# Recurrence of a hybrid decoder layer: loads two chunks ahead, outputs made in loaded tiles, one operand layout for both heads

## The chip, the cores and the metric

The kernel runs on one core of a Trainium2 chip. The metric is the device time of one execution in microseconds (us), the smaller the better. The engines are named as in the profile: PE multiplies matrices, DVE and ACT work on vectors, POOL and SP here mostly issue DMAs. Each engine runs its own list of instructions in order, and semaphores make it wait for the others.

## The reference

One layer of a decoder: token mixing by two branches (RWKV-7 and S5), gated and merged, then an MLP. Sequence 1024, model width 1024, float32. The change is in the RWKV-7 branch, with 8 heads of 64 channels:

```python
def step(S, inp):
    r_t, w_t, k_t, v_t, a_t, b_t = inp
    sa = jnp.einsum('bhij,bhj->bhi', S, a_t)
    S = (S * w_t[:, :, None, :] + sa[..., None] * b_t[:, :, None, :]
         + v_t[..., None] * k_t[:, :, None, :])
    return S, jnp.einsum('bhij,bhj->bhi', S, r_t)
...
y = ((y - mean) * lax.rsqrt(var + LNX_EPS)).reshape(bsz, L, RWKV_WIDTH) * lnx_w + lnx_b
bonus = jnp.sum(rh * kh * r_k, axis=-1, keepdims=True) * vh
y = (y + bonus.reshape(bsz, L, RWKV_WIDTH)) * g
```

## The kernel before

**Chunks.** The recurrence is computed in chunks i = 0 to 3. A chunk is half of the sequence (th = i // 2) for four heads (g = i % 2, as two pairs u = 0, 1), cut into 8 blocks of 64 steps. A chunk goes through these stages, which the text calls by name and number, as in level(1):

- rwkv_front: for each pair u SP and POOL load k, the decay, the rate and r (L693), ACT and DVE form the operands ar, bk and the decay products (L697 to L732), PE forms the block products (L743), DVE masks them into the tile gr (L745), and POOL stores parts of gr to DRAM (md, L751).
- rwkv_inv: POOL loads md as the tile mt (L795), DVE inverts the 32x32 triangles in 31 steps of two instructions (L802 writes tm, L804 the tile x), and POOL stores x (xd, L807) and loads it into gr (L814).
- rwkv_nat: PE transposes bk and v for the chain (L774 to L784).
- rwkv_level: the two 32x32 triangles of a block become one of 64x64. DVE transposes out of gr into a tile xz (L826), PE multiplies (L829, L831), ACT copies back (L830 into xz, L832 into gr).
- rwkv_chain: eight steps one after the other, L859 to L902, each a round of small matmuls with DVE and ACT between them.
- rwkv_out: normalisation (L933 to L943), PE transposes back, factors are loaded (L926), ACT scales (L951), DVE adds and multiplies (L954).

**Fill.** PE does not wait for this: between the pieces it gets matmuls of 128x512 of the projections (L176, L177, L178, three passes for one product, called fill below). In order these are tiles of the gates, then the merge of the first half of the sequence, which needs the outputs of chunks 0 and 1, the output projection, and the gated unit of the S5 branch. Each weight is cast on ACT (L159) and DVE (L160).

**Order.** `drive` (L200 on) runs generators, the lanes, and hands out fill when none is due: chain_lane (L1981) with nat, level, chain and out, prep_lane (L1959) for u = 0 and 1 with front and inv, and glu_lane. Each yields a cost and a due time or a condition, from the table of T constants at L2020. PE keeps the order in which this program writes its instructions. The other engines' lists are ordered by the priorities of the lanes and when operands are planned to be ready. A front of chunk i is started when rwkv_nat(i-1) has been issued.

**Tiles.** Pool "ld" has NLD = 10 places, shared by loaded tiles, the factors, the outputs and xz. The tile x of the inversion has one place, so a second x waits until the first has been stored and read.

```python
x = self.tg("x", 1, (128, 2, 8, 32), pool=self.rka)
...
xz = self.tg("ld", NLD).rearrange("p (u c t) -> p u c t", u=2, t=32)
...
yield 0, lambda: self.nat >= i - 1
```

Of the kernel before, what the change touches and what calls it, by code (L numbers as in the profile page):

```python
# [42 lines left out]
_o = 0  # L43
for _n, _c in (("ident", 128), ("gmask", 192), ("ones_bd", 128), ("nrow", 128),
               ("xinit", 256), ("smask", 512)):
    CST[_n] = (_o, _c)
    _o += _c
# [3 lines left out]
def _constants():  # L51
    c = np.zeros((128, NCST), np.float32)

    def put(name, a):
        o, n = CST[name]
        c[:, o:o + n] = a
    p = np.arange(128)
    put("ident", np.eye(128))
    s, t = (p % 64)[:, None], (p % 64)[None, :]
    g = np.where(p[None, :] < 64, s < t, s <= t)  # L60
    put("gmask", np.concatenate([g, g[:, 0:64]], axis=1))
    put("ones_bd", (p[:, None] // 64) == (p[None, :] // 64))
    put("nrow", np.broadcast_to(p[None, :], (128, 128)))
    x = np.zeros((128, 8, 32))
    for lane in range(128):
        for i in range(8):
            x[lane, i, 4 * i + lane // 32] = 1
    put("xinit", x.reshape(128, 256))
    put("smask", np.broadcast_to((np.arange(512) % 64 != 0)[None, :], (128, 512)))
    return c  # L70


class Kern:
# [591 lines left out]
    def rwkv_tiles(self, d, g, th):  # L665
        d.update(g=g, th=th)
        pool = self.rk if g else self.rka
        d["ar"] = self.tg("ar", 1, (128, 2, 8, 128), pool=pool)
        d["bk"] = self.tg("bk", 1, (128, 2, 8, 128), pool=self.rka)
        d["gr"] = self.tg("gr", 1, (128, 2, 8, 2, 128), pool=pool)  # L670
# [5 lines left out]
    def rwkv_front(self, d, u):  # L676

# [3 lines left out]
        p = 2 * d["g"] + u  # L681
        ar, bk = d["ar"][:, u], d["bk"][:, u]
        ar0, ar1, bk0, bk1 = [[x[HS[h], :, HS[h ^ j]] for h in range(2)] for x in (ar, bk) for j in range(2)]

        gf = d["gr"][:, u].rearrange("p c h t -> p (c h t)")
# [12 lines left out]
        if d["g"] == d["th"] == 0:  # L698
            self.tc.add_manual_dep(self.squared.ins, self.last_wh.ins.name, ORDER)
        yield 0, T_LD  # L700
        st = self.rp((128, 4, 2))
        for tb in range(4):
# [12 lines left out]
        G.tensor_copy(d["pt"][:, :, u], pe[:, :, 64])  # L715
        tk = self.tg("ld", NLD)
        A.activation(tk, ta, AF.Identity, bias=self.ka_1[:, p:p + 1], scale=self.ka_h[:, p:p + 1])
        V.tensor_tensor(tk, tk, k, ALU.mult)
        for h, sl in enumerate(HS):
            V.tensor_tensor(ar1[h], c64(r)[sl], pe[sl, :, 1:65], ALU.mult)  # L720
            V.tensor_tensor(bk1[h], c64(tk)[sl], c64(tz)[sl], ALU.mult)
        yield 0.9, T_KN, 1.5
        kb = self.rp()
# [11 lines left out]

        gm = [self.cst("gmask")[:, x].unsqueeze(1).to_broadcast([128, 4, 128]) for x in (slice(0, 128), slice(64, 192))]
        for q in range(2):
# [6 lines left out]
            for h in range(2):  # L744
                V.tensor_tensor(d["gr"][:, u, 4 * q:4 * q + 4, h], ps[h], gm[h], ALU.mult)  # L745
            yield 1.8, T_GR
        for blk in range(2):
            md = d["md"][u, blk].rearrange("(c h) q t -> h q c t", h=2)
            for h in range(2):
                sl = slice(64 * h + 32 * blk, 64 * h + 32 * blk + 32)  # L750
                nc.gpsimd.dma_start(md[h], d["gr"][sl, u, :, h, sl])  # L751

        V.scalar_tensor_tensor(r, r, self.vec("r_k", p), tk, ALU.mult, ALU.mult)
        pb = self.rp()
# [34 lines left out]
    def rwkv_inv(self, d):  # L789
# [19 lines left out]
        for u in range(2):  # L809
            for blk in range(2):  # L810
                xd = xds[16 * blk:16 * blk + 16, u].rearrange("(c h) s r t -> h (s r) c t", h=2)
                for h in range(2):
                    sl = slice(64 * h + 32 * blk, 64 * h + 32 * blk + 32)
                    nc.gpsimd.dma_start(d["gr"][sl, u, :, h, sl], xd[h])  # L814

    def rwkv_level(self, d):
# [5 lines left out]
        p0, p1 = [p0[:, u] for u in range(2)], [self.chb().rearrange("p (c t) -> p c t", t=32) for u in range(2)]  # L822
        xz = self.tg("ld", NLD).rearrange("p (u c t) -> p u c t", u=2, t=32)
        top, bot = [[slice(64 * h + o, 64 * h + o + 32) for h in range(2)] for o in (0, 32)]
        for h, sl in enumerate(top):
            self.levelled = V.transpose(xz[sl].rearrange("p u c t -> p (u c) t"), gr[sl, :, :, h, sl].rearrange("p u c t -> p (u c) t"))  # L826
        yield 0, T_LT
        kw = dict(stop=True, skip_group_check=True)
        steps = ((lambda u, c, h: mm(p1[u][bot[h], c], gr[top[h], u, c, h, bot[h]], xz[top[h], u, c], start=c == 0, **kw),  # L829
                  lambda u, h: A.copy(xz[bot[h], u], p1[u][bot[h], 0:8])),  # L830
                 (lambda u, c, h: mm(p0[u][top[h], c], xz[bot[h], u, c], gr[bot[h], u, c, h, bot[h]], start=c == 0, **kw),  # L831
                  lambda u, h: A.copy(gr[top[h], u, :, h, bot[h]], p0[u][top[h], 0:8])))  # L832
        for step, evict in steps:
# [10 lines left out]
    def rwkv_chain(self, d):  # L844
# [5 lines left out]
        kw = dict(stop=True, skip_group_check=True)  # L850
        uh = [(u, h, HS[h], HS[1 - h]) for u in range(2) for h in range(2)]

        def banks():
# [3 lines left out]
        def values(pg, c, u):  # L857
            for _, h, sl, ot in uh[0:2]:
                mm(pg[sl, u], gr[ot, u, c, h, sl], UV[ot, (c + h) % 8, h, u], start=u == 0, **kw)  # L859

# [9 lines left out]
        for c in range(8):  # L870
# [4 lines left out]
            for u in range(2):  # L875
                for _, h, sl, ot in uh[0:2]:
                    mm(pa[sl, u], ar[sl, u, c, sl], S[sl, u], start=u == 0, **kw)
                if c < 7:
# [8 lines left out]
            for u, h, sl, ot in uh:  # L887
                mm(pu[sl, u], gr[sl, u, c, h, sl], p1[sl, u], start=u == 0, **kw)
            for u, h, sl, ot in uh:
                mm(py[ot, u], ar[sl, u, c, ot], S[sl, u], start=c == 7 and u == 0, **kw)  # L890
            V.tensor_copy(UV[0:64, c, 0], pu[0:64])
            A.copy(UV[64:128, (c + 1) % 8, 1], pu[64:128])
            yield 0.45, T_CH
            for u, h, sl, ot in uh:
                mm(py[ot, u], gr[:, u, c, h, ot], UV[:, (c + h) % 8, h, u], start=False, **kw)
            o = 64 * (c % 2)
# [17 lines left out]
    def rwkv_out(self, d):  # L914
# [4 lines left out]
        final = th == 1 and d["g"] == 1  # L919
        ts = []  # L920

        def factors(u):
            r = []
            for src in (d["bv"][u], self.TG[2 * d["g"] + u][:, o]):
                t = self.tg("ld", NLD)
                (G if final else nc.sync).dma_start(t, src)  # L926
# [978 lines left out]
    def front_half(self):  # L1905
# [26 lines left out]
        with tc.tile_pool(reuse_waits="tile", name="rk", bufs=1) as self.rk, tc.tile_pool(reuse_waits="tile", name="evb", bufs=NEV) as self.evp, \  # L1932
# [5 lines left out]
            self.leveling, self.masked = False, 0.0  # L1938
            self.fronts = 0
            mg, self.mx0 = [], []  # L1940
# [18 lines left out]
    def prep_lane(self, u):  # L1959
        for i, d in enumerate(self.ds):  # L1960
            yield 0, lambda: self.nat >= i - 1
            if not d:
                self.rwkv_tiles(d, i % 2, i // 2)
            yield from self.rwkv_front(d, u)
            self.fronts += 1
# [15 lines left out]
    def chain_lane(self, mg):  # L1981
# [4 lines left out]
        for i, d in enumerate(self.ds):  # L1986
# [41 lines left out]
NLD = 10  # L2028
# [82 lines left out]
```

## Time and profile before

| | |
|---|---|
| median of 3 runs | 1575.64 us (1575.17 to 1583.24) |
| profiled execution | 1575.62 us, span of the core 1573.8 us |
| busy DVE, ACT, POOL | 1163.3 us (74%), 731.2 us (46%), 181.1 us (12%) |
| granted PE clock, mean | 0.965 of full speed |
| DMA | 224.46 MB, 143 GB/s on the mean |

A profile row reads: engine, line, what is written <- what is read, count, and then busy time. Times in windows and rows are from the start of the span. `[3.59 <-ACT hh L241]` behind a row means that the engine was idle 3.59 us before it, and that ACT's line 241 ended that wait. PE is busy for most of the span, and the recurrence takes the stretch from about 260 to 800 us.

### The profile page before, as it was taken

How to read it: one execution, taken by the hardware profiler on the slowest of the kernel's cores; microseconds unless marked ns; L12 is line 12 of the kernel's file. 1: busy time of each engine (PE TensorE's matmuls, PEld its weight loads, DVE VectorE, ACT ScalarE, POOL GpSimd, SP SyncE). 2: the span in 40 equal slices, each digit the busy share in tenths (PEclk: the TensorE clock that was granted, in tenths of full speed). 3: DMA queues.
4: the chain of work that ended last, by engine and by line, in shares of the span. 5: the costliest groups of instructions: out<-in, count | busy, mean ns of one | idle time of the engine just before them, and what ended most of it. 6: DMA issues, size and time to landing. Idle time of an engine off the chain costs nothing.

```text
span 1573.8 us, 23463 instructions
## 1 busy us (share of the span) xinstructions
PE 1485.4 (94%) x8608; PEld 1196.8 (76%) x8608; DVE 1163.3 (74%) x2130; ACT 731.2 (46%) x1206; POOL 181.1 (12%) x340
## 2 busy tenths in 40 slices
PE   6997999999998989799799999999999999999995
PEld 5786888878676767567578788888888888788774
DVE  7878874747365568786467869788888887698677
ACT  5454543332344365357534546455555555444350
POOL 0022110132221121303100011000000000000000
PEclk9998999999998998899779999999999999999997
DMA  6454344443333174435425666333333336943722
GB/s 198 122 148 131 101 138 131 149 131 115 103 96 137 62 238 143 140 81 169 134 69 193 208 235 200 107 120 103 118 108 114 121 112 203 333 162 129 235 65 107
DMA packets 121123, 224.46 MB, mean 143 GB/s; under 512 B 30976, under 2 KB 37120, under 8 KB 121008
## 3 DMA queue, kind: packets, MB, share of 16 engines
q1 hardware_dynamic: 90144, 154.02, 31.1%
q0 software_dynamic: 21024, 64.71, 12.3%
q10 hardware_dynamic: 9840, 4.24, 1.0%
q8 instruction: 67, 1.10, 0.3%
q14 instruction: 48, 0.39, 0.1%
HBM read 163.41 MB, written 57.41 MB: 140 GB/s over the span
## 4 chain that ended last, share of the span: by engine, by line
PE 71%; DVE 11%; DMA 9%; issue 5%; ACT 3%; SPq 1%; POOL 0%; DVEq 0%; ACTq 0%; POOLq 0%
PE gm L176 10%; PE gm L177 9%; PE gm L178 9%; PE rp L1541 5%; PE rp L1543 5%; PE rp L1542 5%; DMA st<-in_w_down_dram 3%; PE mm L1541 2%; PE mm L1543 2%; PE mm L1542 2%; PE d L1719 1%; PE d L1720 1%; PE d L1718 1%; DVE wl L242 1%; DVE wl L160 1%
## 5 line engine op out<-in xcount | busy, mean ns | idle before, releaser
L176 PE MATMUL gm<-hh,wh 128*128 128x512 f32 x688 | 290.3, 422 | 9.5 <-ACT hh L241 7.1
L177 PE MATMUL gm<-hl,wh 128*128 128x512 f32 x688 | 274.2, 399 | 1.4 <-DVE hl L242 1.2
L178 PE MATMUL gm<-hh,wl 128*128 128x512 f32 x688 | 272.8, 396 | 0.0
L159 ACT CAST wh<-wf 128x512 fp32r<-128x512 f32 x178 | 109.7, 620 | 189.6 <-PE gm L177 111.1
L160 DVE TENSOR_TENSOR wl<-wf,wh 128x512 fp32r<-128x512 f32 x178 | 122.7, 692 | 73.8 <-ACT wh L159 72.8
L176 PEld LDWEIGHTS gm<-hh,wh 128*128 128x128 f32 x688 | 131.7, 191 | 43.3 <-ACT hh L241 9.3
L178 PEld LDWEIGHTS gm<-hh,wl 128*128 128x128 f32 x688 | 131.9, 192 | 28.7
L177 PEld LDWEIGHTS gm<-hl,wh 128*128 128x128 f32 x688 | 132.1, 192 | 27.8 <-DVE hl L242 5.2
L1719 PE MATMUL d<-xl,wh 128*128 128x512 f32 x308 | 120.4, 391 | 5.3 <-DVE xl L242 5.3
L1718 PE MATMUL d<-xh,wh 128*128 128x512 f32 x308 | 120.1, 390 | 0.0
L1720 PE MATMUL d<-xh,wl 128*128 128x512 f32 x308 | 119.9, 389 | 0.0
L1541 PE MATMUL rp<-t,h 128*128 128x512 f32 x252 | 98.3, 390 | 1.6 <-ACT p L1555 1.6
L1542 PE MATMUL rp<-t,h 128*128 128x512 f32 x252 | 98.1, 389 | 0.0
L1543 PE MATMUL rp<-t,l 128*128 128x512 f32 x252 | 98.0, 389 | 0.0
L1719 PEld LDWEIGHTS d<-xl,wh 128*128 128x128 f32 x308 | 57.8, 188 | 19.3 <-DVE xl L242 7.4
L242 DVE TENSOR_TENSOR l<-r,h 128x1024 fp32r<-128x1024 f32 (+1 forms) x40 | 38.9, 972 | 40.0 <-ACT h L241 40.0
L241 ACT CAST h<-r 128x1024 fp32r<-128x1024 f32 (+1 forms) x40 | 34.0, 849 | 72.3 <-PE rp L1542 67.2
L1720 PEld LDWEIGHTS d<-xh,wl 128*128 128x128 f32 x308 | 57.8, 188 | 11.9
L1718 PEld LDWEIGHTS d<-xh,wh 128*128 128x128 f32 x308 | 57.8, 188 | 11.9
L1562 DVE SCALAR_TENSOR_TENSOR y<-zv,vecs,y 128x1023 f32<-128x1023 f32 (+1 forms) x42 | 53.8, 1281 | 10.2 <-ACT y L1560 10.2
L1541 PEld LDWEIGHTS rp<-t,h 128*128 128x128 f32 x252 | 47.3, 188 | 12.2 <-ACT p L1555 2.4
L1543 PEld LDWEIGHTS rp<-t,l 128*128 128x128 f32 x252 | 47.3, 188 | 9.9
(457 smaller groups left out, 3370.3 us busy)
## 6 DMA issues: line engine op xcount, KB each, us to landing
r<-in_w_up_dram SPq DMA_DIRECT2D x42, 512.0 KB, 3.7
wf<-in_w_in_dram SPq DMA_DIRECT2D x72, 256.0 KB, 3.0
st<-in_w_down_dram SPq DMA_DIRECT2D x55, 256.0 KB, 4.7
st<-ACT SPq DMA_DIRECT2D x44, 256.0 KB, 4.4
ACT<-y POOLq DMA_DIRECT2D x21, 512.0 KB, 2.9
GT<-ev POOLq DMA_DIRECT2D x32, 256.0 KB, 3.4
wf<-in_w_br_dram SPq DMA_DIRECT2D x32, 256.0 KB, 3.5
wf<-in_w_out_dram SPq DMA_DIRECT2D x32, 256.0 KB, 2.9
```

Of the source, the lines that this page charges most:

```text
L159: self.last_wh = nc.scalar.copy(h[:, :n], f[:, :n])
L160: nc.vector.tensor_tensor(l[:, :n], f[:, :n], h[:, :n].bitcast(F32), ALU.subtract)
L176: mm(ps, a, xh[k], start=a0, stop=False)
L177: mm(ps, a, xl[k], start=False, stop=False)
L178: mm(ps, b, xh[k], start=False, stop=z0)
L242: self.split_ops = a, (eng or self.nc.vector).tensor_tensor(lo, x, hi.bitcast(F32), ALU.subtract)
L1541: mm(ps, wh[:, c], xh, start=first and k == 0, stop=False, skip_group_check=True)
L1542: mm(ps, wh[:, c], xl, start=False, stop=False, skip_group_check=True)
L1543: mm(ps, wl[:, c], xh, start=False, stop=k == 3, skip_group_check=True)
L1718: mm(ps, wh[:, c], xh[:, x], start=start, stop=False, skip_group_check=True)
L1719: mm(ps, wh[:, c], xl[:, x], start=False, stop=False, skip_group_check=True)
L1720: mm(ps, wl[:, c], xh[:, x], start=False, stop=stop, skip_group_check=True)
```

## The change

1. **Loads.** A front's loads and its first squares are issued when chain(i-2) has been issued (new counter `chains`), and not when nat(i-1) has. The rest of the front still waits for nat(i-1), and for the outputs of chunk i-2, whose loaded factors now lie in the tile ar. For chunks 0 and 1 the new load condition holds from the start.
2. **Operands.** ar and gr have the same column order for both heads, so that the products at L720 and L729 take one instruction for 128 partitions in place of two for 64. The mask is one of 128 columns. The product r*r_k*tk stands earlier, and tk lies in a part of gr in place of a tile of "ld".
3. **Outputs.** Factors are loaded into the dead ar (or "ld") before the transposes, and two DVE instructions read the transposed PSUM tile, add and multiply in place. The scaling on ACT (L951) is gone.
4. **Level.** xz takes the tile x of the inversion (one place) in chunks 0 to 2.
5. **Due times.** T_KN 17 to 12, T_BK 13 to 10, T_INV 62 to 58.

```diff
     def rwkv_tiles(self, d, g, th):
...
+    def rwkv_operands(self, d):
+        d["ar"] = self.tg("ar", 1, (128, 2, 8, 128), pool=self.rk if d["g"] else self.rka)
+        d["bk"] = self.tg("bk", 1, (128, 2, 8, 128), pool=self.rka)
...
         yield 0, T_LD
+        yield 0, lambda: self.nat >= i - 1 and self.outs >= i - 1
+        if "ar" not in d:
+            self.rwkv_operands(d)
...
-        tk = self.tg("ld", NLD)
+        tk = yb
...
+        V.tensor_tensor(ar1, c64(r), pe[:, :, 1:65], ALU.mult)
         for h, sl in enumerate(HS):
-            V.tensor_tensor(ar1[h], c64(r)[sl], pe[sl, :, 1:65], ALU.mult)
             V.tensor_tensor(bk1[h], c64(tk)[sl], c64(tz)[sl], ALU.mult)
+        V.scalar_tensor_tensor(r, r, self.vec("r_k", p), tk, ALU.mult, ALU.mult)
...
-        for h, sl in enumerate(HS):
-            V.scalar_tensor_tensor(ar0[h], c64(kk)[sl], -1.0, pe[sl, :, 0:64], ALU.mult, ALU.mult)
+        V.scalar_tensor_tensor(ar0, c64(kk), -1.0, pe[:, :, 0:64], ALU.mult, ALU.mult)
...
-        V.scalar_tensor_tensor(r, r, self.vec("r_k", p), tk, ALU.mult, ALU.mult)
...
-        xz = self.tg("ld", NLD).rearrange("p (u c t) -> p u c t", u=2, t=32)
+        xz = (self.tg("ld", NLD) if d["g"] and d["th"] else self.tg("x", 1, pool=self.rka)).rearrange("p (u c t) -> p u c t", u=2, t=32)
...
-                t = self.tg("ld", NLD)
+                t = self.tg("ld", NLD) if final or d["g"] > j else free[:, (2 if u == 0 else 0) + j]
...
-            sq = self.tg("ld", NLD, (128, 8, 64))
+            sq = free[:, j].rearrange("p (a i) -> p a i", i=64)
...
+        if not final:
+            ts = [factors(u) for u in range(2)]
         yield 0, T_LF if final else T_LN
...
-            y1 = self.tg("ld", NLD)
-            A.activation(y1, ps.rearrange("p c t -> p (c t)"), AF.Identity, bias=self.vec("lnx_b", p),
-                         scale=self.vec("lnx_w", p))
-            for t, op in zip(ts[u] if final else factors(u), (ALU.add, ALU.mult)):
-                V.tensor_tensor(y1, y1, t, op)
+            y1, tg = ts[u]
+            V.scalar_tensor_tensor(y1, ps.rearrange("p c t -> p (c t)"), self.vec("lnx_w", p), y1, ALU.mult, ALU.add)
+            V.scalar_tensor_tensor(y1, y1, self.vec("lnx_b", p), tg, ALU.add, ALU.mult)
...
     def prep_lane(self, u):
         for i, d in enumerate(self.ds):
-            yield 0, lambda: self.nat >= i - 1
+            yield 0, lambda: self.chains >= i - 1
...
             yield from self.rwkv_chain(d)
+            self.chains = i + 1
...
-T_KN, T_BK, T_GR, T_INV, T_LV, T_CH, T_LN, T_LF = 17.0, 13.0, 2.5, 62.0, 1.0, 0.8, 16.0, 14.5
+T_KN, T_BK, T_GR, T_INV, T_LV, T_CH, T_LN, T_LF = 12.0, 10.0, 2.5, 58.0, 1.0, 0.8, 16.0, 14.5
```

The first place where the order moves is DVE's list around level(0). Before, the inversion of chunk 0 ends with the last write of x_3158, and the two transposes of level(0) (L826, into the tile ld_3781) follow inside the operands of front(1):

```order
596 L802 TENSOR_TENSOR tm_3254<-x_3158,mt_3157 128x16
...
598 L804 TENSOR_TENSOR x_3158<-x_3158,tm_3254 128x16
...
608 L160 TENSOR_TENSOR wl_3797<-wf_3798,wh_3796 128x512
609 L826 STREAM_TRANSPOSE ld_3781<-gr_2606 32x512
610 L732 SCALAR_TENSOR_TENSOR bk_3355<-gr_3356,ld_3371 64x8x64
611 L826 STREAM_TRANSPOSE ld_3781<-gr_2606 32x512
612 L732 SCALAR_TENSOR_TENSOR bk_3355<-gr_3356,ld_3371 64x8x64
```

After the change, DVE's list at the same stage (the transposes of level are L830 now; x_3109 and x_3695 are the inversions of chunks 0 and 1, tm and mt their operands, x_3828 and x_4637 the tiles xz of levels 0 and 1; L885 is the first step of chain(0)):

```order
609 L807 TENSOR_TENSOR x_3109<-x_3109,tm_3205 128x16
...
614 L749 TENSOR_TENSOR gr_3024<-rp_3638,csts 128x4x128
...
619 L805 TENSOR_TENSOR tm_3701<-x_3695,mt_3694 128x62
...
680 L807 TENSOR_TENSOR x_3695<-x_3695,tm_3791 128x16
681 L830 STREAM_TRANSPOSE x_3828<-gr_2604 32x512 x2
...
683 L830 STREAM_TRANSPOSE x_4637<-gr_3024 32x512 x2
684 L713 SCALAR_TENSOR_TENSOR ld_4534<-csts,ld_4534 128x512
...
686 L885 TENSOR_TENSOR p_797_3980<-p_797_3980,chk_3982 128x128
```

The whole of front(1) and of the inversion of chunk 1 now stands ahead of level(0)'s transposes, where before they stood behind them, and the transposes of level(1) and a scan of chunk 2 (L713) stand ahead of chain(0).

The second place is PE's list in the fourth and fifth step of the last chain, chain(3). Before, the steps (chk, chb and p are a step's products, S the state, UV the values) follow each other with nothing between:

```order
2760 L888 MATMUL chb_7927<-p_1509_7899,gr_5878 64x64 x4
2761 L890 MATMUL chk_7926<-S_2601,ar_5876 64x64 x4
2762 L895 MATMUL chk_7926<-UV_7355,gr_5878 64x64 x4
2763 L900 MATMUL chb_7927<-UV_7355,bkn_7354 64x64 x4
2764 L877 MATMUL chk_7964<-S_2601,ar_5876 64x64 x2
2765 L859 MATMUL chk_7964<-UV_7355,gr_5878 64x64 x2
...
2768 L888 MATMUL chb_7965<-p_1513_7937,gr_5878 64x64 x4
```

After the change, in the same chain (L882, L864, L893, L895, L900 and L905 are its products now; gm_7746 and gm_7803 are fill):

```order
2669 L882 MATMUL chk_7768<-S_2601,ar_5729 64x64 x2
2670 L864 MATMUL chk_7768<-UV_6999,gr_5588 64x64 x2
...
2673 L176 MATMUL gm_7746<-e_7152,wh_7737 128x512
2674 L177 MATMUL gm_7746<-e_7153,wh_7737 128x512
2675 L178 MATMUL gm_7746<-e_7152,wl_7738 128x512
...
2679 L893 MATMUL chb_7769<-p_1430_7705,gr_5588 64x64 x4
2680 L895 MATMUL chk_7768<-S_2601,ar_5729 64x64 x4
...
2687 L900 MATMUL chk_7768<-UV_6999,gr_5588 64x64 x4
```

Fill now stands between all products of that chain. From the first product of chain(3) to its end there are 210 fill matmuls in place of 96; counted from the start of the recurrence's fill, nat(0) stands at fill 957 in place of 993, level(0) at 1164 in place of 1233, chain(0) at 1200 in place of 1269 and chain(3) at 1965 in place of 2151, of 2892 in all.

More of the change, by code (lines that the diff above doesn't have):

```diff
@@ L43 @@
 _o = 0
-for _n, _c in (("ident", 128), ("gmask", 192), ("ones_bd", 128), ("nrow", 128),
+for _n, _c in (("ident", 128), ("gmask", 128), ("ones_bd", 128), ("nrow", 128),
                ("xinit", 256), ("smask", 512)):
@@ L60, in _constants @@
     g = np.where(p[None, :] < 64, s < t, s <= t)
-    put("gmask", np.concatenate([g, g[:, 0:64]], axis=1))
+    put("gmask", g)
     put("ones_bd", (p[:, None] // 64) == (p[None, :] // 64))
@@ L666, in rwkv_tiles @@
         d.update(g=g, th=th)
[L667 to L670, printed above, removed]
+        d["gr"] = self.tg("gr", 1, (128, 2, 8, 2, 128), pool=self.rk if g else self.rka)
         d["v"] = {}
@@ L681, in rwkv_front @@
         p = 2 * d["g"] + u
-        ar, bk = d["ar"][:, u], d["bk"][:, u]
-        ar0, ar1, bk0, bk1 = [[x[HS[h], :, HS[h ^ j]] for h in range(2)] for x in (ar, bk) for j in range(2)]
         gf = d["gr"][:, u].rearrange("p c h t -> p (c h t)")
@@ L700, in rwkv_front @@
         yield 0, T_LD
+        yield 0, lambda: self.nat >= i - 1 and self.outs >= i - 1
+        if "ar" not in d:
+            self.rwkv_operands(d)
+        ar, bk = d["ar"][:, u], d["bk"][:, u]
+        ar0, ar1 = ar[:, :, 0:64], ar[:, :, 64:128]
+        bk0, bk1 = [[bk[HS[h], :, HS[h ^ j]] for h in range(2)] for j in range(2)]
         st = self.rp((128, 4, 2))
@@ L734, in rwkv_front @@
         yield 0.5, T_BK
-        gm = [self.cst("gmask")[:, x].unsqueeze(1).to_broadcast([128, 4, 128]) for x in (slice(0, 128), slice(64, 192))]
+        gm = self.cst("gmask").unsqueeze(1).to_broadcast([128, 4, 128])
         for q in range(2):
@@ L744, in rwkv_front @@
             for h in range(2):
-                V.tensor_tensor(d["gr"][:, u, 4 * q:4 * q + 4, h], ps[h], gm[h], ALU.mult)
+                V.tensor_tensor(d["gr"][:, u, 4 * q:4 * q + 4, h], ps[h], gm, ALU.mult)
             yield 1.8, T_GR
@@ L822, in rwkv_level @@
         p0, p1 = [p0[:, u] for u in range(2)], [self.chb().rearrange("p (c t) -> p c t", t=32) for u in range(2)]
-        xz = self.tg("ld", NLD).rearrange("p (u c t) -> p u c t", u=2, t=32)
+        xz = (self.tg("ld", NLD) if d["g"] and d["th"] else self.tg("x", 1, pool=self.rka)).rearrange("p (u c t) -> p u c t", u=2, t=32)
         top, bot = [[slice(64 * h + o, 64 * h + o + 32) for h in range(2)] for o in (0, 32)]
+        t0, t1 = slice(0, 32), slice(32, 64)
         for h, sl in enumerate(top):
-            self.levelled = V.transpose(xz[sl].rearrange("p u c t -> p (u c) t"), gr[sl, :, :, h, sl].rearrange("p u c t -> p (u c) t"))
+            self.levelled = V.transpose(xz[sl].rearrange("p u c t -> p (u c) t"), gr[sl, :, :, h, t0].rearrange("p u c t -> p (u c) t"))
         yield 0, T_LT
         kw = dict(stop=True, skip_group_check=True)
-        steps = ((lambda u, c, h: mm(p1[u][bot[h], c], gr[top[h], u, c, h, bot[h]], xz[top[h], u, c], start=c == 0, **kw),
+        steps = ((lambda u, c, h: mm(p1[u][bot[h], c], gr[top[h], u, c, h, t1], xz[top[h], u, c], start=c == 0, **kw),
                   lambda u, h: A.copy(xz[bot[h], u], p1[u][bot[h], 0:8])),
-                 (lambda u, c, h: mm(p0[u][top[h], c], xz[bot[h], u, c], gr[bot[h], u, c, h, bot[h]], start=c == 0, **kw),
-                  lambda u, h: A.copy(gr[top[h], u, :, h, bot[h]], p0[u][top[h], 0:8])))
+                 (lambda u, c, h: mm(p0[u][top[h], c], xz[bot[h], u, c], gr[bot[h], u, c, h, t1], start=c == 0, **kw),
+                  lambda u, h: A.copy(gr[top[h], u, :, h, t1], p0[u][top[h], 0:8])))
         for step, evict in steps:
@@ L851, in rwkv_chain @@
         uh = [(u, h, HS[h], HS[1 - h]) for u in range(2) for h in range(2)]
+        t0, t1 = HS
         def banks():
@@ L858, in values @@
             for _, h, sl, ot in uh[0:2]:
-                mm(pg[sl, u], gr[ot, u, c, h, sl], UV[ot, (c + h) % 8, h, u], start=u == 0, **kw)
+                mm(pg[sl, u], gr[ot, u, c, h, t0], UV[ot, (c + h) % 8, h, u], start=u == 0, **kw)
         def keep(pg):
@@ L876, in rwkv_chain @@
                 for _, h, sl, ot in uh[0:2]:
-                    mm(pa[sl, u], ar[sl, u, c, sl], S[sl, u], start=u == 0, **kw)
+                    mm(pa[sl, u], ar[sl, u, c, t0], S[sl, u], start=u == 0, **kw)
                 if c < 7:
@@ L887, in rwkv_chain @@
             for u, h, sl, ot in uh:
-                mm(pu[sl, u], gr[sl, u, c, h, sl], p1[sl, u], start=u == 0, **kw)
+                mm(pu[sl, u], gr[sl, u, c, h, t0], p1[sl, u], start=u == 0, **kw)
             for u, h, sl, ot in uh:
-                mm(py[ot, u], ar[sl, u, c, ot], S[sl, u], start=c == 7 and u == 0, **kw)
+                mm(py[ot, u], ar[sl, u, c, t1], S[sl, u], start=c == 7 and u == 0, **kw)
             V.tensor_copy(UV[0:64, c, 0], pu[0:64])
@@ L894, in rwkv_chain @@
             for u, h, sl, ot in uh:
-                mm(py[ot, u], gr[:, u, c, h, ot], UV[:, (c + h) % 8, h, u], start=False, **kw)
+                mm(py[ot, u], gr[:, u, c, h, t1], UV[:, (c + h) % 8, h, u], start=False, **kw)
             o = 64 * (c % 2)
@@ L919, in rwkv_out @@
         final = th == 1 and d["g"] == 1
-        ts = []
+        free = d["ar"].rearrange("p u c t -> p (u c t)").rearrange("p (j t) -> p j t", t=512)
         def factors(u):
             r = []
-            for src in (d["bv"][u], self.TG[2 * d["g"] + u][:, o]):
-                t = self.tg("ld", NLD)
+            for j, src in enumerate((d["bv"][u], self.TG[2 * d["g"] + u][:, o])):
+                t = self.tg("ld", NLD) if final or d["g"] > j else free[:, (2 if u == 0 else 0) + j]
                 (G if final else nc.sync).dma_start(t, src)
@@ L1938, in front_half @@
             self.leveling, self.masked = False, 0.0
-            self.fronts = 0
+            self.fronts, self.chains = 0, 0
             mg, self.mx0 = [], []
@@ L1960, in prep_lane @@
         for i, d in enumerate(self.ds):
-            yield 0, lambda: self.nat >= i - 1
+            yield 0, lambda: self.chains >= i - 1
             if not d:
                 self.rwkv_tiles(d, i % 2, i // 2)
-            yield from self.rwkv_front(d, u)
+            yield from self.rwkv_front(d, u, i)
             self.fronts += 1
```

6 lines of the change are left out of this document (3 added, 3 removed).

## The prediction

> **What bounds the kernel now.** I read the page first, then PE's windows over the recurrence, then the waits of PE.
>
> ```profile
> PE 1485.4 (94%) x8608; PEld 1196.8 (76%) x8608; DVE 1163.3 (74%) x2130; ACT 731.2 (46%) x1206; POOL 181.1 (12%) x340
> ```
>
> PE is busy 94% of the span, so a saving must be idle or slow time of PE. The windows (stretch, its length, then busy time and count of PE, weight loads, DVE, ACT, POOL, then granted clock, DMA share and GB/s) cut the recurrence at its gaps:
>
> ```profile
> 330.00:480.00 150.00, 149.20 (x1164) 114.18 (x1163) 84.79 (x257) 56.69 (x130) 37.44 (x67) 1.00 0.40 115
> 480.00:510.00 30.00, 25.61 (x243) 18.86 (x242) 17.05 (x46) 12.82 (x25) 3.25 (x6) 0.83 0.36 124
> 510.00:580.00 70.00, 69.47 (x646) 51.36 (x646) 37.30 (x89) 30.36 (x78) 15.71 (x30) 1.00 0.41 118
> 580.00:600.00 20.00, 13.53 (x45) 8.85 (x43) 17.41 (x41) 15.97 (x24) 1.91 (x4) 0.66 0.79 277
> 624.00:646.00 22.00, 11.60 (x50) 8.95 (x49) 20.04 (x33) 6.70 (x12) 8.82 (x15) 0.77 0.64 211
> 748.00:760.00 12.00, 7.58 (x59) 5.08 (x58) 5.53 (x9) 5.67 (x12) 1.16 (x3) 0.72 0.43 147
> 770.00:804.00 34.00, 25.82 (x315) 20.59 (x315) 12.52 (x34) 13.63 (x45) 2.75 (x6) 0.60 0.22 77
> ```
>
> I call length minus busy time times clock the loss of a window. In the five windows below clock 1 it is 8.7, 11.1, 13.1, 6.5 and 18.5 us (30 - 25.61 x 0.83, and so on), **57.9 us** in all; the first and third row show under 1 us each. The waits behind these losses, from the timeline (start, length, engine, line, operation, tiles, wait before it):
>
> ```profile
> 497.04 0.64 PE L831 MATMUL chk<-gr,ld 32*32 32x32 f32 x16 [1.99 <-ACT gr L832]
> 585.82 0.80 PE L176 MATMUL gm<-hh,wh 128*128 128x512 f32 x1 [3.59 <-ACT hh L241]
> 641.84 0.59 PE L743 MATMUL rp<-ar,bk 64*128 64x128 f32 x2 [5.59 <-DVE bk L721]
> 752.78 0.64 PE L831 MATMUL chk<-gr,ld 32*32 32x32 f32 x16 [4.05 <-ACT gr L832]
> 774.93 0.45 PE L888 MATMUL chb<-p,gr 64*64 64x64 f32 x8 [2.05 <-DVE p L880]
> ```
>
> In this order they are level(1), the merge's first product, front(3), level(3), and the bare steps of chain(3). Behind the third row's wait DVE is full (20.04 of 22 us), so that place is bound by DVE.
>
> **Gains, part by part.** *Level(1), 8.7.* ACT's copies stood behind front(2)'s loads. These are now issued a stage earlier, and DVE has level(1)'s transposes done before chain(0): I take all of it, bounds 6 to 8.7. *Chain(3), 18.5.* It now has 210 fill matmuls between its products. A step of chain(1) or chain(2) with fill shows the third row's picture (69.47 of 70 us busy at clock 1.00), so I take all of it, bounds 15 to 18.5. *Level(3), 6.5.* Its copies share ACT with the gated unit's work as before, and that order is hardly changed: I take 2.5, bounds 0 to 6.5, so 4 stay.
>
> *Merge and front(3), 24.2 together.* Outputs of chunks 0 and 1 are done earlier, so the merge's values no longer wait for out(1). But DVE has inv(2), out(1) and front(3) in one list between the end of chain(1) and front(3)'s first product, and PE has only its fill beside them.
>
> ```profile
> L804 DVE TENSOR_TENSOR x<-x,tm 128x120 f32<-128x120 f32 (+24 forms) x124 | 32.4, 261 | 2.5
> L802 DVE TENSOR_TENSOR tm<-x,mt 128x120 f32<-128x120 f32 (+24 forms) x124 | 32.3, 260 | 2.3
> L720 DVE TENSOR_TENSOR ar<-ld,gr 64x512 f32<-64x512 f32 x16 | 10.8, 684 | 14.4 <-DMA ld<-RKV 12.4 <-ACT spt L885 1.8
> L142 DVE SCALAR_TENSOR_TENSOR rsy<-rsh,rsy 128x4 f32<-128x4 f32 (+2 forms) x60 | 9.2, 165 | 0.9
> 371.85 0.18 DVE L804 TENSOR_TENSOR x<-x,tm 128x16 f32<-128x16 f32 x1
> 351.80 0.22 DVE L802 TENSOR_TENSOR tm<-x,mt 128x62 f32<-128x62 f32 x1
> ```
>
> An inversion is 16.2 us of rows ((32.4 + 32.3) / 4), and the one of chunk 0, from 351.80 to 372.03, took 20.2 with little beside it; I use 18.5. DVE's list then holds about 29 operations of 512 columns (0.69 us, the L720 row; one of 1024 columns counted as two) and 37 small ones of the rsqrt (some 0.2 with their spacing): 18.5 + 20 + 7.4 = 46, and 4 for the first sums of out(1) ahead: **50 us**. PE in that time has 138 fill matmuls and about 9 us of its own for nat(2), out(1) and front(3).
>
> ```profile
> 738.01 0.39 PE L178 MATMUL gm<-hh,wl 128*128 128x512 f32 x1
> 738.24 0.39 PE L176 MATMUL gm<-hh,wh 128*128 128x512 f32 x1
> 332.21 0.60 PE L774 MATMUL rp<-csts,bk 128*128 128x128 f32 x4
> 397.44 0.44 PE L829 MATMUL chb<-ld,gr 32*32 32x32 f32 x16
> 388.50 1.16 PE L743 MATMUL rp<-ar,bk 64*128 64x128 f32 x16
> ```
>
> Fill starts every 0.228 us (the first two rows), so 138 take 31.4 and PE needs about 41. It waits some 9 us for DVE there, and level(2), right behind it, needs the inversion's round trip through DRAM: 2 more, and about 3 for the slow clock behind such waits. So 14 of the 24.2 stay, bounds 5 and 24. The halved instructions at L720 and L729 (8 fewer each, 0.69 us, 11 us of DVE over four chunks) and the removed ACT scaling are in this sum only where DVE is waited for, which is here: 2.7 us for a chunk, already counted in the 29.
>
> **A new wait at level(0).** xz now shares the one place of x. The order shown above puts inv(1) first, so level(0)'s transposes wait until inv(1) has run and its x is stored. DVE keeps its order, so everything behind stands too: the transposes of level(1), chain(0).
>
> *When PE arrives.* Before, nat(0) stood at 332.21 and level(0) at 397.44: 65.2 us for 240 fill matmuls, nat(0) and part of front(1). Nat(0) now has 36 fill matmuls fewer ahead (8.2 us): 324.0. From there to level(0) there are 207 (7.5 us less), but two groups of L743 (1.16 each) and a pair of L755 (1.0) more: 61. PE arrives at 385, later by what front(1)'s products wait for DVE, which runs inv(0) between their masks: I take 3, bounds 0 and 7 (0 since it hardly waited there before, 7 near the 5.59 above). So 388.
>
> *When the transposes can run.* DMAs on the way, with least, median and most time to landing of mt, and the medians of the other two (behind the size in KB):
>
> ```profile
> DMA to landing us min/median/max: 3.6/6.2/9.3
> xd<-x POOLq DMA_DIRECT2D x16, 64.0 KB, 3.4
> gr<-xd POOLq DMA_DIRECT2D x32, 32.0 KB, 2.8
> 372.32 2.56 POOL L807 DMA_DIRECT2D xd<-x  x4 [2.61 <-DVE x L804]
> 383.90 0.70 DVE L826 STREAM_TRANSPOSE ld<-gr 32x512 f32<-32x512 f32 x1 [1.35 <-DMA gr<-xd]
> ```
>
> The load of mt(1) stands on POOL's queue behind a gate tile's store, whose products end 12 fill matmuls before level(0): 388 - 2.7 = 385.3. With a sigmoid on ACT and two issues on POOL (about 2.3) and 6.2 + 1.6 for the four loads, mt(1) is there at 395.4; inv(1) adds 18.5 (413.9), its four stores 0.3 + 2.56 + 3.4 - 0.6 (419.6), two transposes 1.4 (421). PE waits from 388 to 421: **33 us**. The bounds: mt landing 3 sooner or later, the inversion 16.2 or 20.2, stores landing at 1.9: 27 to 38. No work hides it, since the products behind it on PE's list are fill, but in order.
>
> *The clock.* Behind the 4.05 us before 752.78 this needs a row of its own:
>
> ```profile
> 754.00:756.00 2.00, 2.00 (x20) 1.27 (x19) 0.00 (x0) 0.38 (x2) 0.00 (x0) 0.50 0.01 4
> 756.00:758.00 2.00, 2.00 (x6) 1.53 (x5) 0.00 (x0) 0.34 (x1) 0.00 (x0) 0.50 0.00 0
> 760.00:762.00 2.00, 2.00 (x26) 1.39 (x26) 1.42 (x3) 1.32 (x3) 0.00 (x0) 1.00 0.49 131
> ```
>
> PE runs at 0.50 until about 758.3 though fully busy, some 5.5 us, so such a wait costs 2.7 us more. Level's small products keep PE less busy than that, and 480 to 510 lost 4.4 to the clock (25.61 x 0.17): I take 4, bounds 2 and 5. The Trainium skill, "TensorE: Matmul & The Clock Gate", section "What's actually happening", has full rate back after one busy window of about 3.4 us; by that page the restart costs 1.7 us and the sum below would be 2.3 lower. The trace's 5.5 us at half rate is longer than the page's window.
>
> So the new wait costs 33 + 3 + 4 = **40 us**, bounds 29 to 50. A check against chain(0): its first step was at 414.74 with 1269 fill matmuls done and would be at about 437 with 1200: 22 + 69 x 0.228 = 38.
>
> ```profile
> 414.74 0.27 PE L877 MATMUL chk<-S,ar 64*64 64x64 f32 x2 [0.46 <-ACT p L863]
> ```
>
> **The sum.** Against the profiled run, 1575.6 (the median of the runs is the same): -57.9 of old losses, +40 at level(0), +14 at merge and front(3), +4 at level(3) = 1575.7, so about **1576, no change**: large gains given back at one place.
>
> **The rivals.**
> 1. *Faster: the old losses go and the new wait is at its low end.* If DVE keeps up at front(3) (5 stay) and the pieces of the 29 to 50 end low (33), the time is 1575.6 - 57.9 + 33 + 5 + 4 = 1560. For it: only 4 of the five old waits are DVE's, and DVE loses 11 us of work. Against it: DVE was over 90% busy from 600 to 646 and inv(2), front(3) are not shorter.
> 2. *Slower: the shared x holds up more.* The mechanism is the same wait, with its upper bounds: inv(1) starts only when front(1)'s last masks are stored, and if inv(0), on the same DVE list, pushes those masks back by the 7 us, the wait and everything behind moves; with 48 for it and 22 at front(3), 1575.6 - 57.9 + 48 + 22 + 4 = 1592. It decides from 48 + 18 on, where what returns exceeds the 57.9 by over 8.
> 3. *The loads come no earlier.* The ten places of "ld" set when a load can start; if fronts 2 and 3 find none, level(1) keeps its 8.7 and the merge some 4 of its 11.1 beyond the 14 counted above, while level(0)'s wait stays: about 1588. Against it: outputs, factors, tk and xz no longer take places.
>
> **How the numbers follow.** Forecast 0.40, faster rival 0.28, slower rival 0.24, loads no earlier 0.08. A measurement tells 0.5%, 8 us, from no change. The forecast holds 1566 to 1586 by its middle bounds, and a tenth of its chance (0.04) lies beyond 8 us on either side. Of the last rival half counts as no change, since without level(1)'s 8.7 its time is 1579. So faster 0.28 + 0.04 = 0.32, same 0.32 + 0.04 = 0.36, slower 0.24 + 0.04 + 0.04 = 0.32. The range over the cases is **1555 to 1595**, 5 beyond the faster rival's time and 3 beyond the slower one's.
>
> **What would show it.** A wait of PE of 27 to 38 us ahead of level(0)'s first product (L833), near 388, put down to DVE's transposes (L830), and these directly behind inv(1). Clock 1.00 and no bare steps in chain(3). A wait of front(3)'s products (L747) for DVE of 5 to 15 us in all. No wait at level(1). If DVE runs level(0)'s transposes before inv(1), or if PE reaches level(0) over 8 us later than 388, the sum is wrong and the kernel faster. If the wait is there and chain(3) still has its bare steps, it is slower by some 18 us.

## The result and the profile after

The changed kernel takes 1591.3 us (median of eight executions; seven lie between 1585.7 and 1595.1, the eighth took 7232 and is left out of the ratio) against 1575.5 before: **1.0% slower**, ratio 1.0102, interval 1.0081 to 1.0123. A second set of the same program gave 1591.1, ratio 1.0122 (1.0101 to 1.0144); its profiled execution, 1588.6 us with a span of 1586.6, is the profile used here.

The windows of that profile, cut like those of before (stretch, length, then busy time and count of PE, weight loads, DVE, ACT, POOL, then clock, DMA share, GB/s):

```profile
384.00:432.00 48.00, 14.83 (x116) 10.23 (x114) 19.14 (x66) 4.06 (x8) 11.15 (x20) 0.61 0.26 59
508.00:522.00 14.00, 13.16 (x126) 9.43 (x126) 6.19 (x27) 6.18 (x14) 1.08 (x2) 0.88 0.17 52
600.00:628.00 28.00, 20.41 (x94) 16.35 (x94) 23.20 (x48) 13.68 (x20) 13.10 (x23) 0.88 0.59 178
706.00:746.00 40.00, 31.99 (x268) 23.74 (x265) 28.75 (x52) 23.42 (x46) 6.73 (x14) 0.87 0.44 142
746.00:806.00 60.00, 59.79 (x558) 43.57 (x551) 32.97 (x77) 35.02 (x86) 5.25 (x10) 1.00 0.30 88
806.00:832.00 26.00, 23.38 (x98) 19.00 (x97) 16.48 (x35) 8.83 (x16) 1.07 (x2) 0.87 0.61 204
```

Length minus busy time times clock gives the loss of each. The first row is level(0), and it alone loses 39.0 us; PE's products fill under a third of it. Level(1) (508 to 522) loses 2.4, the merge and front(3) (600 to 628) 10.0, out(2) and level(3) together (706 to 746) 12.2, chain(3) (746 to 806) 0.2, and a sum of squares of the output projection (806 to 832) 5.7. Cut at 728 us, the fourth row is 8.5 us for out(2) and 3.5 for level(3). The timeline of PE shows what it waited for in these places (start, length, engine, line, operation, tiles, wait before it):

```profile
420.05 0.31 PE L833 MATMUL chb<-x,gr 32*32 32x32 f32 x2 [32.74 <-DVE x L830]
623.44 2.04 PE L747 MATMUL rp<-ar,bk 64*128 64x128 f32 x14 [5.53 <-DVE bk L736]
720.83 1.94 PE L956 MATMUL rp<-csts,yn 128*128 128x128 f32 x8 [5.59 <-DVE yn L948]
739.45 0.44 PE L835 MATMUL chk<-gr,ld 32*32 32x32 f32 x16 [1.68 <-ACT gr L836]
821.77 1.36 PE L260 MATMUL rp<-ones,sq 128*128 128x1 f32 x8 [2.62 <-DVE sq L1392]
```

The first is the new wait. What DVE and POOL did meanwhile (the timelines of the two; mt is the operand of inv(1), xd its store):

```profile
386.80 2.13 POOL L798 DMA_DIRECT2D mt<-md  x4
396.19 0.23 DVE L805 TENSOR_TENSOR tm<-x,mt 128x62 f32<-128x62 f32 x1 [7.74 <-DMA mt<-md]
414.46 0.19 DVE L807 TENSOR_TENSOR x<-x,tm 128x16 f32<-128x16 f32 x1
414.94 2.56 POOL L810 DMA_DIRECT2D xd<-x  x4 [26.01 <-DVE x L807]
419.29 1.43 DVE L830 STREAM_TRANSPOSE x<-gr 32x512 f32<-32x512 f32 x2 [4.65 <-DMA xd<-x]
```

Read from top to bottom: the load of mt(1) is issued from 386.80 to 388.9, DVE has it at 396.19, the inversion ends at 414.65, its stores land by 419.29, and only then do level(0)'s transposes run. Their own data (gr of chunk 0) had been on its way since POOL's loads of 375.74 and 379.55. PE stands still from 387.3 to 420.05 for a place in a tile, not for data. The steps of that wait are 8.9 us until mt(1) is there, 18.5 for the inversion, 4.6 for the stores of x, and 0.8 for the first transpose. The first two are spent because DVE's list has inv(1) ahead, which the one place forces here; only the 4.6 us are spent on the place after DVE is free.

### The profile page after: what moved, and what is told of

It is laid out like the page before. It is cut to its first block, busy times and chain, and to the rows that moved or that the text cites. A ratio compares the mean times of both kernels' runs of the same rounds, so it can differ in the third digit from the quotient of the medians.

```text
span 7229.3 us, 23442 instructions
## 1 busy us (share of the span) xinstructions
PE 7168.9 (99%) x8608; PEld 4696.1 (65%) x8608; DVE 1172.4 (16%) x2114; ACT 740.2 (10%) x1196; POOL 179.2 (2%) x340
## 4 chain that ended last, share of the span: by engine, by line
PE 72%; DVE 0%; ACT 0%; issue 0%; DVEq 0%
PE gm L176 7%; PE gm L177 6%; PE gm L178 6%; PE rp L1546 5%; PE rp L1548 5%; PE rp L1547 5%; PE d L1723 4%; PE d L1724 4%; PE d L1725 3%; PE mm L1548 2%; PE mm L1546 2%; PE mm L1547 2%; PE ch L176 2%; PE ch L177 2%; PE ch L178 2%; PE mm L176 2%
## 5 line engine op out<-in xcount | busy, mean ns | idle before, releaser
L176 PE MATMUL gm<-hh,wh 128*128 128x512 f32 x688 | 1217.8, 1770 | 1.5 <-ACT hh L241 1.5
L177 PE MATMUL gm<-hl,wh 128*128 128x512 f32 x688 | 1162.9, 1690 | 0.0
L178 PE MATMUL gm<-hh,wl 128*128 128x512 f32 x688 | 1148.6, 1669 | 0.0
L178 PEld LDWEIGHTS gm<-hh,wl 128*128 128x128 f32 x688 | 615.9, 895 | 276.0 <-issue 271.6
L177 PEld LDWEIGHTS gm<-hl,wh 128*128 128x128 f32 x688 | 646.5, 940 | 211.9 <-issue 211.3
L176 PEld LDWEIGHTS gm<-hh,wh 128*128 128x128 f32 x688 | 582.8, 847 | 258.3 <-issue 254.9
L1723 PE MATMUL d<-xh,wh 128*128 128x512 f32 x308 | 339.0, 1101 | 0.0
L1546 PE MATMUL rp<-t,h 128*128 128x512 f32 x252 | 331.8, 1317 | 1.3 <-ACT p L1560 1.3
L1548 PE MATMUL rp<-t,l 128*128 128x512 f32 x252 | 331.4, 1315 | 0.0
L1547 PE MATMUL rp<-t,h 128*128 128x512 f32 x252 | 329.4, 1307 | 0.0
L1546 PEld LDWEIGHTS rp<-t,h 128*128 128x128 f32 x252 | 154.5, 613 | 104.0 <-issue 98.9
L1547 PEld LDWEIGHTS rp<-t,h 128*128 128x128 f32 x252 | 152.2, 604 | 98.2 <-issue 98.2
```

The lines of the kernel that those rows point to most:

```text
L176: mm(ps, a, xh[k], start=a0, stop=False)
L177: mm(ps, a, xl[k], start=False, stop=False)
L178: mm(ps, b, xh[k], start=False, stop=z0)
L1546: mm(ps, wh[:, c], xh, start=first and k == 0, stop=False, skip_group_check=True)
L1547: mm(ps, wh[:, c], xl, start=False, stop=False, skip_group_check=True)
L1548: mm(ps, wl[:, c], xh, start=False, stop=k == 3, skip_group_check=True)
```

## The experiments

**Theory S:** the slowdown is the shared place of x, in an order that lets inv(1) take it before level(0). **Rival D:** DVE, full at the merge, front(3) and out(2), is what costs.

**1. The changed kernel again**, unaltered, for the profile above.

> The changed kernel itself, unaltered, to get a readable profile. Theory S (the shared place of x): PE waits 27 to 38 us at level(0)'s first product, put down to DVE's transposes (L830), and the old five losses of 57.9 us fall to about 18. Rival D (DVE at the merge and front(3)): the wait at level(0) is under 15 us and the time lost at merge, front(3) and level(2) is over 30 us. Time near the 1591 already measured, within 8.

Measured 1591.1, and the wait of 32.74 us. The old five losses are down to some 16 (level(1) 2.4, merge and front(3) 10.0, level(3) 3.5, chain(3) 0.2), close to the 18 expected. What was not expected are 8.5 us at out(2) and 5.7 at the sum of squares, where the kernel before loses nearly nothing.

**2. Level(0) gets its own tile.**

```diff
-        xz = (self.tg("ld", NLD) if d["g"] and d["th"] else self.tg("x", 1, pool=self.rka)).rearrange(...)
+        xz = (self.tg("x", 1, pool=self.rka) if d["g"] != d["th"] else self.tg("ld", NLD)).rearrange(...)
```

> One edit: xz of level(0) is a tile of ld again, the rest of the change stays. DVE's list then has level(0)'s transposes ahead of inv(1). Theory S: the wait at level(0) goes but for what inv(0)'s own round trip costs (under 5 us), time 1591 - 30 to 40, so 1550 to 1562. Rival D: under 10 us of gain, 1580 or more.

Measured 1556.0, ratio to before 0.989 (0.9854 to 0.9927): 35 us less than the changed kernel, and 1.1% faster than before. PE's list is the same, instruction for instruction; on DVE level(0)'s transposes now stand ahead of inv(1), which runs beside chain(0). In its trace the transposes run inside the stretch where PE has fill, and level(0)'s first product waits for nothing (DVE's row, then PE's):

```profile
387.05 0.70 DVE L830 STREAM_TRANSPOSE ld<-gr 32x512 f32<-32x512 f32 x1 [1.53 <-DMA gr<-xd]
392.46 0.44 PE L833 MATMUL chb<-ld,gr 32*32 32x32 f32 x16
```

Theory S stands; rival D falls as the cause of the slowdown. No run keeps inv(1) ahead on DVE's list and gives level(0) its own tile, so what that order alone would cost is not measured.

**3. The place stays shared, the due times go back.**

```diff
-T_KN, T_BK, T_GR, T_INV, ... = 12.0, 10.0, 2.5, 58.0, ...
+T_KN, T_BK, T_GR, T_INV, ... = 17.0, 13.0, 2.5, 62.0, ...
```

> One edit: T_KN, T_BK, T_INV back to 17, 13, 62; xz stays in the shared x. The program then writes level(0) ahead of inv(1), so x is taken by level(0) first. Theory S: no wait of over 10 us at level(0), time 1555 to 1572. Rival D: what is lost lies later, time 1580 or more.

Measured 1557.8, ratio 0.9914 (0.988 to 0.9947). PE reaches level(0) at 402.10 with no wait before it. So sharing does no harm in the other order: it hurts together with the due times. These times also move other instructions, on PE's list too, so the run is not a test of one place alone.

**4. The place stays shared, the loads go back.**

```diff
-            yield 0, lambda: self.chains >= i - 1
+            yield 0, lambda: self.nat >= i - 1
```

> One edit: the loads of a front are again issued when nat(i-1) is, all else of the change stays. Level(0) again stands ahead of inv(1). Theory S: no long wait at level(0), but level(1)'s 8.7 us come back and part of the merge's, time 1562 to 1578. Rival L (the early loads themselves cost, by their transfers or places): faster than the changed kernel by over 30 us, below 1560.

Measured 1562.2, ratio 0.9932 (0.991 to 0.9953): in the range of theory S, at its low end, 2 us above the rival's bound. Here too level(0) is ahead of inv(1) in DVE's list, and its wait is gone: the early loads are the third thing, with the sharing and the due times, without which the wait does not arise. What theory S said of the rest was partly wrong: level(1)'s 8.7 us did not come back (some 2 to 3 lost there), while PE waits 8.1 us for ACT's copies into gr in front(3) (L731 for L729).

**5. The kernel before with the shared place alone** (xz takes x in chunks 0 to 2, nothing else).

> The kernel before with one edit: xz takes the one place of x in chunks 0 to 2. DVE's list keeps level(0)'s transposes ahead of inv(1). Theory S (sharing costs only where inv(1) takes the place first): no wait over 5 us at level(0) and the time of before within 8 us, 1565 to 1581. Rival P (sharing the place costs by itself): slower than before by 20 us or more.

Measured 1570.1, ratio 0.9959 (0.9941 to 0.9976): not slower, even 0.4% faster; the loss at level(1) fell from 8.4 to 4.1 us in 2-us windows. Rival P falls.

**6. Level(0)'s own tile and the old due times.** Edits 2 and 3 together.

> The changed kernel with level(0)'s own tile and the old due times 17, 13, 62. Theory S: with the old times there was no wait at level(0) to remove, so the same as the run with the old times alone (1557.8), within 5 us. Rival (sharing costs a few us at any order): faster than it by over 8 us.

Measured 1559.9, ratio 0.9873 (0.9834 to 0.9912), against 1557.8 in experiment 3: the same. Where the order is right, the tile is worth nothing, as theory S has it.

**7. One due time.** The changed kernel with T_KN 17.

> The changed kernel with one number put back, T_KN 17 in place of 12; x stays shared, T_BK 10, T_INV 58. DVE's list then has level(0)'s transposes ahead of inv(1). Theory S: the 33 us go with that order, 1550 to 1562. Rival (the due times act by more than this order): over 1570, or below 1545.

Measured 1566.5, ratio 0.9955 (0.9931 to 0.998). A miss of 4 us for theory S, and outside the rival's bounds as well. Its level(0) runs at 395.02 with no wait, so the 33 us are gone with one number; but the profile has about 17 us of loss at the merge, front(3) and level(2) (588 to 626), against some 9.6 in experiment 2 (574 to 598). Due times move what stands beside what; between the versions without the wait at level(0), that came to some 10 us (1556.0 to 1566.5).

**8. The operand layout alone, on the kernel before** (L720 and L729 one instruction for both heads, mask of 128 columns, nothing else).

> The kernel before with the operand layout alone (one instruction for both heads at two places, one mask). DVE loses 11 us of work. If DVE's work counts only where it is waited for (the merge and front(3)): 2 to 6 us faster than before, 1567 to 1571. Rival (all of DVE's work counts): 11 us faster, 1562. Rival (nothing): the same as before.

Measured 1571.2, ratio 0.9974 (0.9953 to 0.9996), 4 us by the ratio, with an interval from under 1 to 7 us. That fits the first case; it excludes 11 us, and no gain only barely. Its profile, of a slower execution (1574.8), shows the saving where it was expected and lost again elsewhere: front(3) loses 7.7 us (622 to 648) in place of 13.5 before, the merge 16.2 (578 to 608) in place of 11.9, at a granted clock of 0.60 in place of 0.77. Why the clock stayed low there is open.

**9. Later transposes of the outputs** (experiment 2 with T_LN 24).

> The changed kernel with level(0)'s own tile (1556 above) and T_LN 24 in place of 16, so that PE comes later to the transposes of the outputs. In the run above PE lost 7.5 us ahead of out(2)'s transposes. If that wait is only a matter of when PE comes: 4 to 8 us faster, 1548 to 1552. Rival (DVE is full in that stretch, the wait moves to the next product): 1553 to 1560 with the loss elsewhere.

Measured 1551.4, ratio 0.9832 (0.9783 to 0.988). This tells nothing of the idea: the number moves no instruction on any engine, and the wait ahead of out(2)'s transposes is again 5.6 us. It is a second measurement of experiment 2's program, whose eight executions thus lie between 1541 and 1562. Differences of 4 us between single runs of these kernels are not told apart.

**10. More work for DVE, at two places.** Experiment 2's kernel, with the product at L723 written eight times in one front:

```diff
-        V.tensor_tensor(ar1, c64(r), pe[:, :, 1:65], ALU.mult)
+        for _ in range(8 if i == 3 else 1):
+            V.tensor_tensor(ar1, c64(r), pe[:, :, 1:65], ALU.mult)
```

> The changed kernel with level(0)'s own tile, and in front(3) alone the product at L723 is written eight times (same values): 14 more DVE instructions of 0.69 us, 9.6 us. PE's list is unaltered. If DVE bounds the stretch from chain(1)'s end to level(2), as the prediction has it: the wait of PE there grows by 8 to 12 us and so does the time, from about 1554 (two runs of that program, 1556 and 1551) to 1562 to 1566. Rival (that wait is a matter of the inversion's DMAs): under 4 us.

> The same 14 instructions in front(2) alone, where DVE is about half busy. If DVE costs only where it is waited for: under 4 us, 1550 to 1558. Rival (every DVE instruction counts): the same 8 to 12 us as in front(3).

In front(3): 1562.5, ratio 0.9918 (0.9891 to 0.9945). In front(2): 1559.4, ratio 0.9892 (0.9855 to 0.993). The windows over the merge and front(3), first of experiment 2's kernel, then of the one with more work in front(3):

```profile
574.00:600.00 26.00, 19.18 (x97) 15.08 (x96) 19.73 (x40) 13.65 (x20) 12.24 (x22) 0.87 0.67 197
```

```profile
574.00:606.00 32.00, 18.03 (x76) 14.76 (x77) 25.36 (x46) 13.44 (x20) 9.96 (x17) 0.73 0.46 127
```

The loss is 9.3 us in the first and 18.8 in the second: 9.6 us of DVE work cost 9.5, and the median is in the range expected. PE now waits 11.9 us for ACT's copy (L730, the line L729 of before this edit), which itself waits for DVE, and 4.7 for DVE's bk. In front(2) the same work left that stretch at 9.5 and raised the loss around level(1) (464 to 496) to 6.5. Experiment 2's profile has 4.3 there, but its repetition (experiment 9) and the run with more work in front(3), with the same instructions up to there, have 0.9. So the work in front(2) costs between 2 and 6 us: less than in front(3), but not nothing. Its median of 1559.4 is a miss against the 1550 to 1558 expected, and its ratio is that of experiment 2. DVE bounds front(3), and front(2) at most in part; the medians alone, with overlapping intervals, would not have shown it.

**11. POOL takes work off DVE** (experiment 2's kernel):

```diff
-        V.tensor_tensor(tk, tk, k, ALU.mult)
-        V.tensor_tensor(ar1, c64(r), pe[:, :, 1:65], ALU.mult)
+        (G if i == 3 else V).tensor_tensor(tk, tk, k, ALU.mult)
+        (G if i == 3 else V).tensor_tensor(ar1, c64(r), pe[:, :, 1:65], ALU.mult)
...
-        self.nc.vector.tensor_tensor(t, t, first, ALU.add)
+        (self.nc.vector if th else self.nc.gpsimd).tensor_tensor(t, t, first, ALU.add)
```

> The changed kernel with level(0)'s own tile, and work taken off DVE where it is full: POOL does the two products at L722 and L723 in front(3) (2.8 us of DVE) and the eight sums of the first merge (5.5 us). PE's list is unaltered. If the waits ahead of front(3)'s products and of out(2)'s transposes (5.0 and 5.6 us in that kernel) are DVE's: they fall to 2 to 4 and 0 to 3, and the time by 4 to 8, to 1546 to 1550. Rival (POOL is slower and its DMAs stand behind it): the same or slower, with new waits for POOL.

Measured 1557.1, ratio 0.9881 (0.9854 to 0.9909): no gain. The groups by line of POOL, and PE's waits at the two places:

```profile
L1232 POOL TENSOR_TENSOR ev<-ev,hl 128x512 f32<-128x512 f32 x8 | 12.0, 1498 | 30.0 <-DVE ev L1227 26.3 <-DVE lm L939 3.6
L723 POOL TENSOR_TENSOR ar<-ld,gr 128x512 f32<-128x512 f32 x2 | 4.0, 2040 | 1.8 <-DVE ld L959 1.8
```

```profile
602.65 2.03 PE L747 MATMUL rp<-ar,bk 64*128 64x128 f32 x14 [4.23 <-DVE ld L759]
680.54 0.32 PE L784 MATMUL rp<-csts,ld 128*64 128x128 f32 x1 [1.85 <-ACT bkn L778]
690.07 1.06 PE L956 MATMUL rp<-csts,yn 128*128 128x128 f32 x8 [3.36 <-DVE yn L948]
```

The rival was right: PE loses 1.85 us at nat(3), and front(3) waits elsewhere. The wait at out(2) falls from 5.59 to 3.36, but not because DVE is done sooner. Its normalisation takes from 672.12 to 689.92, 17.8 us, against 16.9 in experiment 2 (673.14 to 690.08); PE only comes later. DVE's timeline shows why the eight sums fewer did not help:

```profile
674.96 1.57 DVE L247 SCALAR_TENSOR_TENSOR hl<-ev,hh 128x512 fp32r<-128x512 f32 x1
682.87 1.22 DVE L142 SCALAR_TENSOR_TENSOR rsy<-rsh,rsy 128x16 f32<-128x16 f32 x1
687.43 1.23 DVE L142 SCALAR_TENSOR_TENSOR rsy<-rsh,rsy 128x16 f32<-128x16 f32 x1
```

In experiment 2 these take 0.69, 0.18 and 0.18 us. Each begins while POOL is in one of its sums (674.68 to 675.97, 682.75 to 684.04, 687.06 to 688.64) and ends about when that sum does, or later by its own length. POOL takes 1.3 to 2.0 us for what DVE does in 0.69, and beside its twelve products and sums nine DVE instructions are held up in this way, by 7.8 us in all, against the 8.3 us of work taken off DVE. So this run does not test whether DVE's sums are the cause at out(2).

## Why the prediction was right, and where its sum was off

The forecast was no change at 1576. The time is 15 us above it: inside the range, but by the prediction's own measure of 8 us slower, a side that it gave a chance of 0.32. The mechanism at level(0) was right, and the sum missed terms elsewhere.

- **The new wait at level(0): right.** Predicted: PE arrives at 388 and waits until 421, 33 us. Measured: 387.3 to 420.05, 32.74 us. The steps hold one by one to within 1.1 us: mt at 395.4 (396.19), inv(1) over at 413.9 (414.65), stores landed at 419.6 (419.29). That the sum is right to 0.3 us is luck, since mt came 0.8 later and the stores took 4.6 us in place of 5.7. With 1.8 for front(1)'s products and 39.0 for the window it costs 40.8 (predicted 40). Experiment 2 takes 35 of them back. Experiments 3, 4 and 7 remove the wait with x still shared, level(0) ahead of inv(1), and experiment 5 shows that sharing without this order does no harm.
- **The clock: a little more than taken.** After the wait PE ran at half rate for about 10 us:

```profile
396.00:416.00 20.00, 0.00 (x0) 0.00 (x0) 16.35 (x62) 0.00 (x0) 1.06 (x2) 0.50 0.00 0
420.00:424.00 4.00, 3.53 (x36) 2.51 (x37) 0.70 (x1) 0.35 (x1) 4.00 (x8) 0.50 0.21 42
424.00:426.00 2.00, 2.00 (x20) 1.20 (x19) 0.00 (x0) 0.38 (x2) 0.43 (x1) 0.50 0.25 48
426.00:428.00 2.00, 2.00 (x20) 1.19 (x20) 0.00 (x0) 0.10 (x1) 0.00 (x0) 0.50 0.00 0
428.00:430.00 2.00, 2.00 (x6) 1.57 (x7) 0.31 (x1) 1.56 (x4) 0.00 (x0) 0.55 0.00 0
430.00:432.00 2.00, 2.00 (x24) 1.35 (x22) 0.38 (x1) 0.37 (x1) 0.58 (x1) 1.00 0.23 57
```

  That is a loss of some 5 us, where I took 4. The Trainium skill ("TensorE: Matmul & The Clock Gate", "What's actually happening") has the full rate back after at least one busy window of about 3.4 us. One such window, an estimate of 1.7 us of loss, was too little here: the 10 us are about three. In this stretch level's small products stand between the fill; whether they are the reason, no run shows.
- **Chain(3): right.** Its 18.5 us are gone (0.2 left). **Level(1):** 2.4 of 8.7 stay, where I had none.
- **Merge and front(3): right in kind and a little too high.** Predicted 14 to stay, measured 10.0. That DVE is the bound there is shown by experiment 10, for the kernel of experiment 2.
- **Level(3): right in size, by other neighbours.** 3.5 us stay where 4 were taken. But the order there did change: ACT's copies stand among the merge's casts (L246, L1204) and no longer among the output projection's (L1382, L1385).
- **The step that failed: terms put at nothing.** The prediction lists only the five old places. It has no term for out(2), which loses 8.5 us to the wait ahead of its transposes and the slow clock behind it, and none for the sum of squares behind chain(3), which loses 5.7. PE waited at neither place before. With level(1)'s 2.4 that is 16.6 us too little, less the 4 too much at the merge: 12.6, of the 13 us by which the profiled execution (1588.6) lies above the forecast.
- **A misreading.** The faster rival counts four of the five old waits as DVE's. The rows show two, at front(3) and chain(3); the other three are put down to ACT.

For out(2) DVE's order suggests the cause, though no run shows it. Before, out(2) ran beside the output projection and its normalisation took from 719.11 to 729.5, 10.4 us; after, chain(2) comes 168 fill matmuls earlier, beside the second half of the merge, which gives DVE three operations a tile (L1227, L1232, L247), and it takes from 703.73 to 720.7, 17.0 us (first the two rows of before, then those of after):

```profile
719.11 1.22 DVE L933 TENSOR_REDUCE lm<-yn 128x16 f32<-128x1024 f32 x1
728.32 1.23 DVE L943 TENSOR_TENSOR yn<-yn,rsy 128x1024 f32<-128x1024 f32 x1
```

```profile
703.73 1.22 DVE L938 TENSOR_REDUCE lm<-yn 128x16 f32<-128x1024 f32 x1
719.46 1.23 DVE L948 TENSOR_TENSOR yn<-yn,rsy 128x1024 f32<-128x1024 f32 x1
```

The prediction goes by how far each stage moves along the fill, and not by which fill then stands beside it. Experiment 11, meant to test this, could not. The sum of squares (L260) had no run of its own. It loses 5.9 us in experiment 2 and under 1 in the repetition of that program, so these 5.7 us are in part the chance of one execution, and what decides there is open.

Of the rivals, the slower one came near the time (1592) by another way than its own: level(0) cost 41 and not 48, and front(3) 10 and not 22. That the loads come no earlier did not happen.

The best version is the change with level(0)'s own tile: 1556.0 and 1551.4 in two measurements, 1.1% and 1.7% faster than before.

## What to carry to other kernels

A tile with one place is a lock, and whoever is written first takes it: before sharing it, look at which of the two users stands first on the engine's list, for every due time that the planner may use. When a change shifts stages against the background work, list what then stands beside each stage on each engine, since a stage that waited for nothing may meet heavier work. A full engine costs at the place where it is waited for: the same 9.6 us of DVE work cost PE 9.5 us in one front and 2 to 6 in another. And work handed from DVE to POOL is not off DVE for free: here 7.8 of 8.3 us came back as DVE instructions that were held up.

## What was not expected of the hardware

The granted clock stayed at 0.50 for about 10 us after PE had started again (420 to 430), nearly twice as long as the 5.5 us behind the wait of 4 us before the change. DVE instructions of 0.18 us took 1.2 when they began beside a sum on POOL. And one program, measured on two chips, spread over 20 us (1541 to 1562) in eight executions; its two profiles, 18.8 us apart, part in several steps, the largest some 5 us at the sum of squares.
